# A hybrid attention block on one core: small VectorE instructions rewritten with per-partition scalars, and one DMA issued by another engine

## The chip, the core and the metric

The kernel runs on one core of a Trainium2 chip. That core has TensorE (PE, with PEld for its weight loads), VectorE (DVE), ScalarE (ACT), GpSimd (POOL) and SyncE (SP). Each takes its own stream of instructions in order; they wait for one another through semaphores. DMAs are issued by an engine as one more instruction of its stream: here SP issues most, ACT the rest. The metric is the device time of one execution in microseconds (us), lower is better.

## The reference, cut to what matters

One decoder layer, float32, 2048 tokens, width 1024. After an input projection come 8 forgetting-transformer heads ("fox", 64 wide) and 8 latent-attention heads ("mla", 96 wide for scores, 64 for values), both causal; then an output projection, a squared-ReLU MLP and a final RMSNorm.

```python
def rmsnorm(x, g):
    x32 = x.astype(jnp.float32)
    y = x32 * lax.rsqrt(jnp.mean(x32 * x32, axis=-1, keepdims=True) + EPS)
    return (y * g.astype(jnp.float32)).astype(x.dtype)
...
        logits = jnp.einsum('bhqd,bhkd->bhqk', q_blk, k).astype(jnp.float32) * scale
...
        p = jax.nn.softmax(logits, axis=-1).astype(v.dtype)
        return jnp.einsum('bhqk,bhkd->bhqd', p, v)
```

Two pieces matter here: the softmax of each 128-query row block, whose denominator is a sum of two chunk sums when a row has more than 1024 keys, and the rsqrt of each RMSNorm.

## The kernel before

**Stages.** By the trace: input projection and per-head operand preparation up to about 520 us; attention from about 550 to 1400 us; output projection to about 1650 us; MLP; and final norm to the end.

**Attention.** Units of 512 queries of one head are worked through in the order fox, mla, fox, mla. Three streams of steps are laid over each other by a queue with due times (`SLACK`, `BEHIND`, `STORE`), and a scheduler that simulates the program then sets each engine's order of instructions. For each 128-query tile, PE makes scores (L872), DVE masks them and takes the negative maximum (L877/L880), ACT takes the exponential with its row sum (L881). If a row has two key chunks, `norm` takes their common minimum (L893), two correction factors `fac` on ACT (L894), the sum of `lsum*fac` (L897, L898) and its reciprocal (L899) on DVE; POOL scales the probabilities (L902).

The value product follows: PE transposes four 128x128 blocks of probabilities into one PSUM tile (L922), and `split_ps` divides it into a high part by ACT (L104) and a low part by DVE (L105). PE multiplies the values with the high part (L939) and the low part (L940). So every 512-column product waits for ACT and then for DVE.

**The result of a unit.** The product matrix holds two 64-row parts that are to be added. ACT copies the PSUM result to `o1` (L944); a DMA shifts rows 64 to 127 of it to partitions 0 to 63 of `o2` (L945: "the shift", 128 KB, within SBUF); POOL adds (L950); a DMA stores `o2` to `mixT` (L951). `o2` is one of two buffers, `halves`, taken in turn, so the shift of unit n overwrites the tile that the store of unit n-2 reads, and must wait for that store to land. Shift, store and all loads of the next heads' operands (L197 to L219) are in the stream of SP. A mla head's load is eight DMAs (L206 to L209, twice) into buffers that PE must be done with.

**Norms.** `rstd` computes a reciprocal square root by POOL's power (L80) and one refinement on DVE (L82 to L86), for one column (w=1) or two (w=2).

Of the kernel before, what the change touches and what calls it, by code (L numbers as in the profile page):

```python
# [18 lines left out]
P = 128  # L19
# [26 lines left out]
def block_kernel(ctx, tc, x, positions, attn_norm_g, w_in, b_forget, q_norm_g, w_uq, kv_norm_g, w_ukv,  # L46
# [29 lines left out]
    def rstd(ssq, n, w=1, tag=""):  # L76
        v = sml.tile([P, 4], F32, name=f"rs_v{tag}")[:, 0:w]
        nc.vector.tensor_scalar(v, ssq, 1.0 / n, EPS, ALU.mult, ALU.add)  # L78
        y = sml.tile([P, 4], F32, name=f"rs_y{tag}")[:, 0:w]
        nc.gpsimd.tensor_tensor(y, v, mhalf[:, 0:w], ALU.pow)  # L80
        t = sml.tile([P, 4], F32, name=f"rs_t{tag}")[:, 0:w]
        nc.vector.tensor_tensor(t, y, y, ALU.mult)  # L82
        nc.vector.tensor_tensor(t, t, v, ALU.mult)  # L83
        nc.vector.tensor_scalar(t, t, -0.5, 1.5, ALU.mult, ALU.add)  # L84
        r = sml.tile([P, 4], F32, name=f"rs_r{tag}")[:, 0:w]
        nc.vector.tensor_tensor(r, y, t, ALU.mult)  # L86
        return r

    def rstd_pool(ssq, n, w=1, tag=""):
# [721 lines left out]
    with ExitStack() as es:  # L811
# [36 lines left out]
        def score_steps(head, qb, st):  # L848

            ops, _ = head  # L850
            nch = qb // 2 + 1
            st["p"] = [[] for _ in range(QB)]
            negm = sma.tile([P, QB, nch], F32, name=f"negm{nch}")
            lsum = sma.tile([P, QB, nch], F32, name=f"lsum{nch}")
            fac = sma.tile([P, QB, nch], F32, name=f"fac{nch}")
            steps = []

            def step(j, c):
                t = QB * qb + j
                k0, k1 = cuts(t)[c]  # L860
                w = k1 - k0
                prob = mid([P, 1024])
                st["p"][j].append((k0, prob))
                nb = 1 if w <= 512 else 2
                wb = w // nb
                ps = pss.tile([P, 2, 512], F32, name="ps_s")
                qs = slice(t * P, (t + 1) * P)
                wm = max(wb, 256)
                for i in range(nb):
                    kb = k0 + i * wb  # L870
                    for n, (l, r, rows) in enumerate(ops):
                        nc.tensor.matmul(ps[:, i, 0:wm], l[0:rows, qs], r[0:rows, kb:kb + wm], start=(n == 0),  # L872
                                         stop=(n == len(ops) - 1))
                src = ps[:, 0:nb, 0:wb]
                if c == nch - 1:

                    nc.vector.tensor_tensor_reduce(src, src, maskb[:, 1024 - w:].rearrange("p (b w) -> p b w", b=nb),  # L877
                                                   -1.0, -NEG, ALU.add, ALU.min, negm[:, j, c:c + 1])
                else:
                    nc.vector.tensor_reduce(negm[:, j, c:c + 1], src, AX.XY, ALU.max, negate=True)  # L880
                nc.scalar.activation(prob[:, 0:w].rearrange("p (b w) -> p b w", b=nb), src, AF.Exp,  # L881
                                     scale=-1.0 if c == nch - 1 else 1.0,
                                     bias=negm[:, j, c:c + 1], accum_out=lsum[:, j, c:c + 1])
                if c == nch - 1:
                    norm(j)

            def norm(j):
                rl = sma.tile([P, 1], F32, name="rl")
                if nch == 1:
                    nc.vector.reciprocal(rl, lsum[:, j])  # L890
                else:
                    m = sma.tile([P, 1], F32, name="mmin")
                    nc.vector.tensor_reduce(m, negm[:, j], AX.X, ALU.min)  # L893
                    nc.scalar.activation(fac[:, j], negm[:, j], AF.Exp, scale=-1.0, bias=m)  # L894
                    l2 = sma.tile([P, nch], F32, name=f"l2{nch}")
                    l1 = sma.tile([P, 1], F32, name="l1")
                    nc.vector.tensor_tensor(l2, lsum[:, j], fac[:, j], ALU.mult)  # L897
                    nc.vector.tensor_reduce(l1, l2, AX.X, ALU.add)  # L898
                    nc.vector.reciprocal(rl, l1)  # L899
                for c, (k0, k1) in enumerate(cuts(QB * qb + j)):  # L900
                    pr = st["p"][j][c][1][:, 0:k1 - k0]
                    nc.gpsimd.tensor_scalar(pr, pr, rl, 1.0 if nch == 1 else fac[:, j, c:c + 1], ALU.mult, ALU.mult)  # L902

            for j in range(QB):
                for c in range(nch):
                    steps.append(lambda j=j, c=c: step(j, c))
            return steps

        def value_steps(head, row0, qb, st):
            _, v = head  # L910
            nk = QB * qb + QB
            steps = []

            parts = {}

            def step(kt):
                j0 = max(0, kt - QB * qb)
                o0 = j0 * P
                ps = pspt.tile([P, 512], F32, name="ps_t")
                for j in range(j0, QB):  # L920
                    k0, prob = [p for p in st["p"][j] if p[0] <= kt * P][-1]
                    nc.tensor.transpose(ps[:, j * P:(j + 1) * P], prob[:, kt * P - k0:(kt + 1) * P - k0], ident)  # L922
                if len(due) == 3:
                    due[0]()
                n = turns[0] = (turns[0] + 1) % 3
                hi, lo = place[2 * n], place[2 * n + 1]
                split_ps(hi[:, o0:], lo[:, o0:], ps[:, o0:])
                parts[kt] = hi, lo, o0

                due.append(lambda: product(kt))  # L930

            def product(kt):
                if kt not in parts:
                    return
                due.pop(0)
                if kt == 0:
                    st["o"] = pspt.tile([P, 512], F32, name="ps_t")
                hi, lo, o0 = parts.pop(kt)
                nc.tensor.matmul(st["o"][:, o0:], v[:, kt, :], hi[:, o0:], start=(kt == 0), stop=False)  # L939
                nc.tensor.matmul(st["o"][:, o0:], v[:, kt, :], lo[:, o0:], start=False, stop=(kt == nk - 1))  # L940
                if kt == nk - 1:
                    n = outs[0] = 1 - outs[0]
                    o1, o2 = f32v(place[6 + n]), halves[n]
                    nc.scalar.activation(o1, st["o"], AF.Copy)  # L944
                    nc.sync.dma_start(o2, o1[HD:P])  # L945
                    st["out"] = o1, o2

            def store():
                o1, o2 = st["out"]
                pin(nc.gpsimd.tensor_tensor(o2, o2, o1[0:HD], ALU.add))  # L950
                nc.sync.dma_start(mixT[row0:row0 + HD, qb * 512:(qb + 1) * 512], o2)  # L951

            for kt in range(nk):
                steps.append((lambda kt=kt: step(kt), lambda kt=kt: product(kt)))
            return steps, store
# [529 lines left out]
        return ss  # L1485

    def fin_b(b, half, j, cl, cr, ss):
        nc.vector.tensor_tensor(ss[:, 0:1], ss[:, 0:1], ss[:, 1:2], ALU.add)  # L1488
        r = rstd(ss[:, 0:1], D)
        r0 = 1024 * b + 512 * half + P * j  # L1490
        for side, t in ((0, cl), (1, cr)):
            nc.vector.scalar_tensor_tensor(t[:, j], t[:, j], r, g_f[:, 512 * side:512 * side + 512], ALU.mult, ALU.mult)  # L1492
            nc.scalar.dma_start(out[r0:r0 + P, 512 * side:512 * side + 512], t[:, j])
        if j == 3:
            s8.put(cl, cr)
# [11 lines left out]
    def finish_rows(half, j, at):  # L1507
        rs = slice(512 * half + P * j, 512 * half + P * (j + 1))
        t, r = [], []

        def load():
            t.append(s4.get([P, 1024], F32))
            nc.sync.dma_start(t[0], y0[rs, :])

        def squares():
            ss = sml.tile([P, 2], F32, name="fin_ss")
            for h in range(2):
                nc.scalar.activation(junk, t[0][:, 512 * h:512 * (h + 1)], AF.Square, accum_out=ss[:, h:h + 1])
            r.append(ss)

        def scale():
            ss, = r
            nc.vector.tensor_tensor(ss[:, 0:1], ss[:, 0:1], ss[:, 1:2], ALU.add)
            nc.vector.scalar_tensor_tensor(t[0], t[0], rstd(ss[:, 0:1], D), g_f, ALU.mult, ALU.mult)

        def store():
            nc.sync.dma_start(out[rs, :], t[0])
            s4.put(t[0])

        for n, f in zip((0, 1, 2, 2.5), (load, squares, scale, store)):  # L1530
            when(at + n, f)
# [130 lines left out]
```

## Time and profile before

| | us |
|---|---|
| median of 3 runs | 2899.03 (2896.02 to 2899.87) |
| the profiled execution, its own time | 2889.38 |
| its span, first to last instruction | 2887.5 |
| PE busy | 2782.5 (96%) |
| VectorE busy | 2164.2 (75%) |
| ScalarE busy | 1431.7 (50%) |
| GpSimd busy | 1378.0 (48%) |

The shares are means over stages with different limits; a stage is read from its own stretch. "PEclk" is the granted TensorE clock as a share of full speed, so 0.50 is 1.2 GHz and 1.00 is 2.4 GHz.

### The profile page before, as it was taken

To read this page: it belongs to the slowest core of one execution; us is meant where nothing else is said; L and a number is where in the kernel's file an instruction comes from. 1 tells how busy PE (TensorE), PEld (TensorE's weight loads), DVE (VectorE), ACT (ScalarE), POOL (GpSimd) and SP (SyncE) were. 2 spreads that over 40 slices of the span, in tenths; PEclk is the share of its full clock that TensorE was granted. 3 is DMA by queue.
4 is the path that set the end of the run, shared out by engine and by line. 5 is a ranking of instruction groups with operands and counts; after the bars stand their busy time and mean duration, and the time that the engine had idled before them with its cause. 6 is when DMAs were issued, how large, how long until landed. Compare 5 with 4: busy or idle time off the path is not lost. (4 is left out here: it accounts for less than half of the span.)

```text
span 2887.5 us, 40299 instructions
## 1 busy us (share of the span) xinstructions
PE 2782.5 (96%) x14378; PEld 2366.3 (82%) x14378; DVE 2164.2 (75%) x3313; ACT 1431.7 (50%) x2533; POOL 1378.0 (48%) x1020
## 2 busy tenths in 40 slices
PE   8999999899999999999899999999999999999998
PEld 7878978788888888888778788887887888878886
DVE  6567466588889989989577766676666687997898
ACT  5344352488888888887433332233223433333432
POOL 2726373355555555556532265656556233453421
PEclk9999999899999999999999999999999999999999
DMA  4554544835335344422345644456346744464551
GB/s 140 185 191 164 172 176 155 218 77 123 88 92 116 93 105 112 93 67 61 113 168 194 248 172 160 146 209 227 141 153 225 248 152 152 163 216 172 188 197 59
DMA packets 262968, 442.61 MB, mean 153 GB/s; under 512 B 42416, under 2 KB 150832, under 8 KB 256048
## 3 DMA queue, kind: packets, MB, share of 16 engines
q1 hardware_dynamic: 207296, 300.42, 35.5%
q10 hardware_dynamic: 55472, 139.61, 12.6%
q8 instruction: 114, 1.87, 0.3%
q14 instruction: 86, 0.70, 0.1%
HBM read 275.21 MB, written 156.37 MB: 149 GB/s over the span
## 5 line engine op out<-in xcount | busy, mean ns | idle before, releaser
L1319 PE MATMUL mm<-big,mid 128*128 128x512 f32 x2688 | 614.8, 390 | 3.1 <-ACT big L1394 2.5
L1319 PEld LDWEIGHTS mm<-big,mid 128*128 128x128 f32 x2688 | 504.0, 188 | 112.6 <-ACT big L1394 7.1
L139 PE MATMUL mm<-big,mid 128*128 128x512 f32 x1312 | 513.2, 392 | 8.9 <-DVE mid L248 6.3
L138 PE MATMUL mm<-big,big 128*128 128x512 f32 (+2 forms) x1160 | 436.1, 376 | 2.7 <-DVE big L248 1.7
L872 PE MATMUL ps_s<-big,big 96*128 96x384 f32 (+11 forms) x1720 | 415.8, 366 | 5.8 <-ACT mid L881 5.7
L902 POOL TENSOR_SCALAR mid<-mid,rl,fac 128x768 f32<-128x768 f32 (+4 forms) x256 | 258.4, 1019 | 336.8 <-DVE rl L899 114.7
L137 PE MATMUL mm<-big,big 128*128 128x512 f32 (+2 forms) x1072 | 402.7, 376 | 1.0 <-ACT big L247 1.0
L247 ACT ACTIVATE big<-mid 128x1024 fp32r<-128x1024 f32 x218 | 214.9, 1050 | 316.1 <-PE mm L138 198.0
L881 ACT ACTIVATE mid<-ps_s,negm 128x896 f32<-128x896 f32 (+7 forms) x384 | 332.6, 866 | 59.9 <-DVE negm L877 47.1
L254 POOL TENSOR_TENSOR mid<-mid,mid 128x1024 f32<-128x1024 f32 x88 | 242.8, 2759 | 232.6 <-DVE mid L248 90.5
L922 PE MATMUL ps_t<-ident,mid 128*128 128x128 f32 x2176 | 341.7, 274 | 8.7 <-POOL mid L902 8.3
L922 PEld LDWEIGHTS ps_t<-ident,mid 128*128 128x128 f32 x2176 | 275.2, 142 | 64.0 <-POOL mid L902 10.0
L872 PEld LDWEIGHTS ps_s<-big,big 96*128 96x128 f32 (+2 forms) x1720 | 287.6, 191 | 28.5 <-ACT mid L881 9.2
L1230 POOL TENSOR_TENSOR mid<-mid,mid 128x1024 f32<-128x1024 f32 x60 | 199.0, 3343 | 230.0 <-DVE big L248 206.1
L139 PEld LDWEIGHTS mm<-big,mid 128*128 128x128 f32 x1312 | 247.6, 189 | 63.0 <-DVE mid L248 7.1
L105 DVE TENSOR_TENSOR big<-ps_t,big 128x512 fp32r<-128x512 f32 (+3 forms) x427 | 255.0, 604 | 50.0 <-ACT big L104 46.5
L248 DVE TENSOR_TENSOR mid<-mid,mid 128x1024 fp32r<-128x1024 f32 x112 | 193.2, 1753 | 117.5 <-ACT mid L247 84.3
L104 ACT ACTIVATE big<-ps_t 128x512 fp32r<-128x512 f32 (+3 forms) x427 | 224.6, 536 | 82.2 <-PE ps_t L922 78.2
L138 PEld LDWEIGHTS mm<-big,big 128*128 128x128 f32 x1160 | 219.8, 189 | 39.5 <-DVE big L248 2.6
L877 DVE CUSTOM_DVE_ANT_0 ps_s<-ps_s,maskb 128x768 f32<-128x768 f32 (+7 forms) x256 | 228.2, 892 | 20.1 <-PE ps_s L872 17.8
L137 PEld LDWEIGHTS mm<-big,big 128*128 128x128 f32 x1072 | 203.5, 190 | 33.7 <-ACT big L247 1.9
L247 ACT ACTIVATE mid<-mid 128x1024 fp32r<-128x1024 f32 x112 | 114.2, 1055 | 209.6 <-POOL mid L254 85.1
(227 smaller groups left out, 5309.4 us busy)
## 6 DMA issues: line engine op xcount, KB each, us to landing
gd<-mid ACTq DMA_DIRECT2D x109, 512.0 KB, 2.7
mid<-gd SPq DMA_DIRECT2D x109, 512.0 KB, 4.4
mid<-in_w_up SPq DMA_DIRECT2D x64, 512.0 KB, 5.8
mid<-in_w_down SPq DMA_DIRECT2D x64, 512.0 KB, 4.6
mid<-in_x SPq DMA_DIRECT2D x32, 512.0 KB, 4.0
xd<-mid ACTq DMA_DIRECT2D x28, 512.0 KB, 6.0
big<-xd SPq DMA_DIRECT2D x14, 1024.0 KB, 5.3
mid<-in_w_in SPq DMA_DIRECT2D x24, 512.0 KB, 5.5
```

The costliest lines, as they stand in the source:

```text
L105: nc.vector.tensor_tensor(lo, ps, f32v(hi), ALU.subtract)
L137: nc.tensor.matmul(ps, lh, rh, start=(k == 0), stop=False)
L138: nc.tensor.matmul(ps, lh, rl, start=False, stop=False)
L139: nc.tensor.matmul(ps, ll, rh, start=False, stop=(k == nk - 1))
L247: nc.scalar.activation(hi, raw, AF.Copy)
L254: (eng or nc.gpsimd).tensor_tensor(t, raws[a], raws[b], op)
L872: nc.tensor.matmul(ps[:, i, 0:wm], l[0:rows, qs], r[0:rows, kb:kb + wm], start=(n == 0), stop=(n == len(ops) - 1))
L877: nc.vector.tensor_tensor_reduce(src, src, maskb[:, 1024 - w:].rearrange("p (b w) -> p b w", b=nb), -1.0, -NEG, ALU.add, ALU.min, negm[:, ...
L881: nc.scalar.activation(prob[:, 0:w].rearrange("p (b w) -> p b w", b=nb), src, AF.Exp, scale=-1.0 if c == nch - 1 else 1.0, bias=negm[:, j, ...
L902: nc.gpsimd.tensor_scalar(pr, pr, rl, 1.0 if nch == 1 else fac[:, j, c:c + 1], ALU.mult, ALU.mult)
L922: nc.tensor.transpose(ps[:, j * P:(j + 1) * P], prob[:, kt * P - k0:(kt + 1) * P - k0], ident)
L1319: nc.tensor.matmul(ps[:, m], l[:, k, tk(m)], r[:, :, tk(k)], start=(first and k == n == 0), stop=(k == 3 and n == 2), skip_group_check=True)
```

## The change

Two edits. First, small VectorE instructions that took two tensors (`tensor_tensor`) become `tensor_scalar` instructions, which take one tensor and up to two per-partition scalars (a 128x1 column each). Second, the shift is issued by ScalarE in place of SyncE. Lines of the changed kernel are 3 higher from the end of `rstd` on (L944/L945 become L947/L948, L951 becomes L954, L104 becomes L107, L881 becomes L884).

```diff
@@ rstd
         t = sml.tile([P, 4], F32, name=f"rs_t{tag}")[:, 0:w]
-        nc.vector.tensor_tensor(t, y, y, ALU.mult)
-        nc.vector.tensor_tensor(t, t, v, ALU.mult)
+        r = sml.tile([P, 4], F32, name=f"rs_r{tag}")[:, 0:w]
+        cols = [slice(c, c + 1) for c in range(w)]
+        for c in cols:
+            nc.vector.tensor_scalar(t[:, c], y[:, c], y[:, c], v[:, c], ALU.mult, ALU.mult)
         nc.vector.tensor_scalar(t, t, -0.5, 1.5, ALU.mult, ALU.add)
-        r = sml.tile([P, 4], F32, name=f"rs_r{tag}")[:, 0:w]
-        nc.vector.tensor_tensor(r, y, t, ALU.mult)
+        for c in cols:
+            nc.vector.tensor_scalar(r[:, c], t[:, c], y[:, c], None, ALU.mult)
         return r
@@ norm, in the attention
-                    l2 = sma.tile([P, nch], F32, name=f"l2{nch}")
+                    l0 = sma.tile([P, 1], F32, name="l0")
                     l1 = sma.tile([P, 1], F32, name="l1")
-                    nc.vector.tensor_tensor(l2, lsum[:, j], fac[:, j], ALU.mult)
-                    nc.vector.tensor_reduce(l1, l2, AX.X, ALU.add)
+                    nc.vector.tensor_scalar(l0, lsum[:, j, 0:1], fac[:, j, 0:1], None, ALU.mult)
+                    nc.vector.tensor_scalar(l1, lsum[:, j, 1:2], fac[:, j, 1:2], l0, ALU.mult, ALU.add)
                     nc.vector.reciprocal(rl, l1)
@@ product, the last key tile of a unit
                     nc.scalar.activation(o1, st["o"], AF.Copy)
-                    nc.sync.dma_start(o2, o1[HD:P])
+                    nc.scalar.dma_start(o2, o1[HD:P])
@@ fin_b and finish_rows, alike
-        nc.vector.tensor_tensor(ss[:, 0:1], ss[:, 0:1], ss[:, 1:2], ALU.add)
+        nc.vector.tensor_scalar(ss[:, 0:1], ss[:, 0:1], ss[:, 1:2], None, ALU.add)
```

SP's stream before, at the load of the third mla head (mq, mr, mk and krd are the head's operands in DRAM): eight loads, the store L951 of an earlier unit ahead of the last of them, then two shifts.

```order
L206 DMA big_9438<-mq_79 64x2048
L207 DMA big_9438<-mr_81 32x2048
L208 DMA big_9439<-mk_83 64x2048
L209 DMA big_9439<-krd_77 32x16x128
L206 DMA big_9440<-mq_80 64x2048
L207 DMA big_9440<-mr_82 32x2048
L208 DMA big_9441<-mk_84 64x2048
L951 DMA mixT<-mid_4985 64x512
L209 DMA big_9441<-krd_78 32x16x128
L945 DMA mid_4985<-mid_4984 64x512 x2
```

The same place in the changed kernel: the store stands behind all eight loads, and there is no shift in this stream any more.

```order
L209 DMA big_9430<-mq_79 64x2048
L210 DMA big_9430<-mr_81 32x2048
L211 DMA big_9431<-mk_83 64x2048
L212 DMA big_9431<-krd_77 32x16x128
L209 DMA big_9432<-mq_80 64x2048
L210 DMA big_9432<-mr_82 32x2048
L211 DMA big_9433<-mk_84 64x2048
L212 DMA big_9433<-krd_78 32x16x128
L954 DMA mixT<-mid_4977 64x512 x3
L218 DMA big_9434<-mv 128x16x128
```

ScalarE's stream before, a few instructions after those loads are due: the copy of a unit's result (L944), and behind it splits (L104) and exponentials (L881).

```order
L944 ACTIVATE mid_4984<-ps_t 128x512 [waits DMAHW1_49,PE_49,Pool_49]
L104 ACTIVATE big_4982<-ps_t 128x512 [waits DVE_49,PE_49]
L881 ACTIVATE mid_8480,lsum_8374<-ps_s,negm_8373 128x1024 [waits DVE_49]
L104 ACTIVATE mid_4983<-ps_t 128x512 [waits PE_49,Activation_49]
L881 ACTIVATE mid_8528,lsum_8526<-ps_s,negm_8525 128x128 [waits DVE_49]
```

The same place after: copy, two exponentials, then the shift, which waits on two DMA semaphores (DMAHW3 is raised by the store L954 that follows the eight loads, DMAHW4 by the load of mk ahead of it), and behind it the next splits (L107).

```order
L947 ACTIVATE mid_4976<-ps_t 128x512 [waits DMAHW1_49,PE_49,Pool_49]
L884 ACTIVATE mid_8472,lsum_8366<-ps_s,negm_8365 128x1024 [waits DVE_49]
L884 ACTIVATE mid_8520,lsum_8518<-ps_s,negm_8517 128x128 [waits DVE_49]
L948 DMA mid_4977<-mid_4976 64x512 [waits DMAHW4_49,DMAHW3_49,Activation_49]
L107 ACTIVATE big_4974<-ps_t 128x512 [waits PE_49]
L107 ACTIVATE mid_4975<-ps_t 128x512 [waits PE_49]
L107 ACTIVATE big_4974<-ps_t 128x512 [waits DVE_49,PE_49]
L884 ACTIVATE mid_8529,lsum_8518<-ps_s,negm_8517 128x256 [waits DVE_49]
```

These two pieces stand in the same form at six mla head loads. What moved: the store slid behind one more load, and the shift went from a stream of DMAs into one whose next rows are compute.

## Rows read from the trace of the kernel before

**Rows 1.** Windows by stage: from:to, length, busy of PE/PEld/DVE/ACT/POOL, PEclk, DMA share, GB/s.

```profile
520.00:600.00 80.00, 65.58 (x375) 56.45 (x374) 55.76 (x139) 45.84 (x108) 29.19 (x33) 0.87 0.66 173
...
800.00:1000.00 200.00, 198.93 (x1231) 174.77 (x1231) 178.24 (x458) 165.30 (x382) 107.26 (x110) 1.00 0.43 100
...
1200.00:1405.00 205.00, 194.85 (x1160) 168.31 (x1159) 173.32 (x408) 158.66 (x350) 119.38 (x111) 0.98 0.27 72
1405.00:1650.00 245.00, 230.57 (x1111) 191.29 (x1110) 174.49 (x307) 90.03 (x125) 77.55 (x72) 0.98 0.54 186
```

**Rows 2.** Groups by line on VectorE: count, ns min/median/max, first and last start.

```profile
L897 DVE TENSOR_TENSOR l<-lsum,fac x128: 134/155/3540, 550.4 to 1389.1; 128x2 f32<-128x2 f32 x128
...
L898 DVE TENSOR_REDUCE l<-l x128: 139/146/155, 550.6 to 1392.3; 128x1 f32<-128x2 f32 x128
...
L82 DVE TENSOR_TENSOR rs_t<-rs_y x48: 148/159/2345, 1410.1 to 2882.2; 128x1 f32<-128x1 f32 x32, 128x2 f32<-128x2 f32 x16
...
L84 DVE TENSOR_SCALAR rs_t<-rs_t x48: 141/155/706, 1410.5 to 2882.6; 128x1 f32<-128x1 f32 x32, 128x2 f32<-128x2 f32 x16
...
L78 DVE TENSOR_SCALAR rs_v<-ssq x16: 141/154/156, 1446.1 to 1635.6; 128x1 f32<-128x1 f32 x16
```

**Rows 3.** Timeline of VectorE, 1342:1349: start, length, instruction, [idle before <- releaser].

```profile
1344.21 3.54 DVE L897 TENSOR_TENSOR l<-lsum,fac 128x2 f32<-128x2 f32 x1 [0.75 <-ACT fac L894]
```

**Rows 4.** Timeline of GpSimd, 1340:1350.

```profile
1344.29 1.11 POOL L968 TENSOR_SCALAR mid<-mid,go 128x1024 f32<-128x1024 f32 x1
1345.37 2.35 POOL L970 TENSOR_TENSOR big<-mid,big 128x1024 fp32r<-128x1024 f32 x1
```

**Rows 5.** Waits of 1325:1405: engine and line, who released it, us in total, times, longest.

```profile
PE ps_t L940 <- DVE big L105: 6.7, 5, 3.2
```

**Rows 6.** Windows around two PE stalls (columns as in rows 1).

```profile
1349.00:1354.00 5.00, 5.00 (x24) 4.35 (x24) 4.86 (x9) 2.76 (x6) 5.00 (x5) 0.69 0.13 30
...
1393.00:1398.00 5.00, 4.67 (x17) 3.95 (x18) 2.66 (x5) 1.22 (x2) 5.00 (x4) 0.66 0.14 45
...
1411.00:1417.00 6.00, 3.59 (x22) 2.63 (x21) 5.45 (x6) 2.78 (x5) 3.08 (x2) 1.00 0.67 219
```

**Rows 7.** Timeline of SyncE's DMA queue, 798:822.

```profile
800.48 0.46 SPq L206 DMA_DIRECT2D big<-mq  x1
...
805.16 0.62 SPq L951 DMA_DIRECT2D mixT<-mid  x1
805.83 0.58 SPq L209 DMA_DIRECT2D big<-krd  x1
806.97 9.83 SPq L945 DMA_DIRECT2D mid<-mid  x2
```

**Rows 8.** Waits of SyncE's queue over the span.

```profile
SPq L945 <- DMA mixT<-mid: 71.2, 14, 10.5
```

**Rows 9.** Timeline of ScalarE, 808:819.

```profile
810.13 0.60 ACT L944 ACTIVATE mid<-ps_t 128x512 f32<-128x512 f32 x1 [0.41 <-issue]
811.04 0.60 ACT L104 ACTIVATE big<-ps_t 128x512 fp32r<-128x512 f32 x1 [0.31 <-PE ps_t L922]
```

**Rows 10.** Timeline of PE, 808:819.

```profile
809.88 0.45 PE L872 MATMUL ps_s<-big,big 128*128 128x256 f32 x2
...
812.25 0.47 PE L939 MATMUL ps_t<-big,big 128*128 128x512 f32 x1
```

**Rows 11.** Timeline of ScalarE and its DMA queue, 1751:1766.

```profile
1753.38 8.38 ACTq L1325 DMA_DIRECT2D gd<-mid  x4
1761.81 1.03 ACT L1394 ACTIVATE big<-mm 128x1024 f32<-128x1024 f32 x1 [7.45 <-DVE mid L1338]
```

**Rows 12.** Timeline of GpSimd, 565:575.

```profile
569.50 1.25 POOL L950 TENSOR_TENSOR mid<-mid,mid 64x512 f32<-64x512 f32 x1 [8.13 <-DMA mid<-mid]
```

**Rows 13.** Timeline of PE, 571:573.

```profile
571.77 0.47 PE L922 MATMUL ps_t<-ident,mid 128*128 128x128 f32 x1 [7.05 <-POOL mid L902]
```

**Rows 14.** Window after that wait (columns as in rows 1).

```profile
572.00:577.00 5.00, 5.00 (x19) 4.52 (x19) 2.37 (x4) 3.23 (x7) 2.73 (x5) 0.50 0.11 25
```

More of the change, by code (lines that the diff above doesn't have):

```diff
@@ L1522, in scale @@
             ss, = r
-            nc.vector.tensor_tensor(ss[:, 0:1], ss[:, 0:1], ss[:, 1:2], ALU.add)
+            nc.vector.tensor_scalar(ss[:, 0:1], ss[:, 0:1], ss[:, 1:2], None, ALU.add)
             nc.vector.scalar_tensor_tensor(t[0], t[0], rstd(ss[:, 0:1], D), g_f, ALU.mult, ALU.mult)
```

## The prediction

> **What bounds the kernel now.** I first read the busy times by stage. In attention PE works 198.9 of the 200 us from 800, ScalarE 165, VectorE 178 [rows 1]. PE is the bound there; ScalarE has some 17% of slack and VectorE 11%. Any time for which PE stands still in this stage is lost for good, since PE never has a reserve to catch up with. At the edges it stands still more: 14.4 of 80 us at the start, 10.2 of 205 at the end of attention, 14.4 of 245 in the output projection [rows 1]. So the question is not how busy VectorE or SyncE are, but which of their waits reach PE.
>
> Next, the groups of small VectorE instructions. The two-tensor forms have a normal median but a long tail: 155 ns and up to 3540 for `l` (L897), 159 and up to 2345 in `rstd` (L82) [rows 2]. The reduction of the same `l`, one input, never goes over 155 ns, and a one-column tensor_scalar never over 156 (L78) [rows 2]. The longest stall, 3.54 us at 1344.2, lies exactly over two large GpSimd instructions that end at 1347.7 [rows 3, 4]. So a two-tensor instruction waits for GpSimd to be done, and one input does not.
>
> Last, SyncE's queue. At 800.5 it starts a mla head's eight loads, issues a store behind seven of them at 805.2, then a pair of shifts that keep it until 816.8 [rows 7]. The second shift waits for that store to land, which only happens when the load data ahead of it has gone through; over the span such waits come to 71.2 us in 14 [rows 8]. On SyncE this costs nothing: what stands behind it are more DMAs, not needed yet.
>
> **The change, part by part.** My sum is made against the profiled execution's own time, 2889.4 us, of which 2887.5 is the span. The median shown is 2899.0, 0.3% more; I put the sum of the changes onto the median.
>
> *Small instructions.* Counts and lengths hardly move: `norm` stays at two instructions (128 calls), one-column `rstd` loses one of four, and the 16 two-column calls gain one, 16 x 0.155 = 2.5 us of VectorE in a stage where it is busy 174 of 245 us, so it is hidden. If that cover were gone it would cost the 2.5 us. What matters is whether the tail goes. If it does:
> - At the end of attention the low-part split stands behind the stalled `l`, and PE's product behind the split: 6.7 us in five waits [rows 5]. The next 5 us are run partly at 1.2 GHz, with a granted clock of 0.69 and 0.66 [rows 6], another 5 x 0.31 + 5 x 0.34 = 3.3 us. At 1411 to 1417 PE loses 2.4 us [rows 6], where a two-column `rstd` is stalled. Together 12; bounds 0 (another wait ends there as late) and 14.
> - In steady attention PE loses only about 1 us in 200 to everything [rows 1]. Over some 780 us of it that is 4; I take half as such stalls' share: -2, bounds 0 and -4.
> - In the output projection 14.4 us are lost to many causes [rows 1]; I give the `rstd` stalls -3, bounds 0 and -6. The final norm's stalls have no PE wait that I can price: 0.
>
> The Trainium skill (SBUF — State Buffer, Who interferes with whom) says that a VectorE instruction with two SBUF inputs contends with GpSimd's reads, and one with at most one does not outside the two-port modes; the trace agrees with the 3.54 us. The same section lets tensor_scalar enter such a mode, which speaks against the edit where operands allow it. That is rival D.
>
> *The shift on ScalarE.* SyncE is relieved of 64 issues at no gain to PE. ScalarE gets 64 more instructions with waits, and ScalarE's rows behind them are splits and exponentials that PE needs. That an engine's DMA holds its own compute is in the trace: ScalarE's DMAs L1325 keep their place from 1753.4 to 1761.8, and the copy behind them starts at 1761.8, long after VectorE had made its data [rows 11]. Most of the 64 shifts wait for nothing that is late. Those at six mla loads do. There the store stands in the changed order behind all eight loads, and the shift, two exponentials after its copy, waits for the store.
>
> The price of one, from the load at 800: the copy ends at 810.13 + 0.60 = 810.73 [rows 9], the shift could go at 806.97 + 9.83 - 0.48 (one issue) = 816.3 [rows 7], so 5.6 us later. In the changed kernel the store has one more load ahead of it, and the copy has some ten more PE instructions between it and the loads; I set these two off against each other. Behind the shift come 0.3 us of issue (estimated from the 0.46 to 0.62 us of one issue in rows 7) and a split of 0.60 [rows 9] before PE can go on: 6.5 us after the copy. PE has work in the meantime: the stretch from 809.88 to 812.25 [rows 10], then two score tiles more by the order, about 1 us at 0.45 a pair, so until 2.5 us after the copy. PE idle: 6.5 - 2.5 = 4.0 us. Stalls of this size were followed by about 1.6 us lost to the lower clock [rows 6]. So 5.6 a load, 34 for six. Bounds: 2.0 (no lower clock, PE running 2 us longer on what is ready) gives 12; 7.7 (idle 6, when the extra load is not set off, plus 1.7) gives 46.
>
> *The first unit.* Before, GpSimd's add waited 8.13 us for the first shift [rows 12], PE stood for 7.05 behind it [rows 13] and then ran 5 us at 0.50 [rows 14], 2.5 us lost: 9.5. After, that shift is not queued behind SyncE's loads, but by the order ScalarE meets a semaphore of such a load right behind the first copy and is held about as long as above. 5.6 - 9.5 = -4, bounds -9 and +4.
>
> Sum: 34 - 4 - 12 - 2 - 3 = **+13**. That is 2902 on the execution's own base, and 2899 + 13 = **2912 us** on the median.
>
> **Rivals.**
> - **A, faster: ScalarE's waits don't reach PE.** If PE has 4 us more of ready work at each load, or the store lands before the copy, the blocks cost nothing and the gains stand alone: -12 - 2 - 3 = -17, and up to -9 more at the first unit: 2873 to 2882, with partial blocks up to 2893. For it: ScalarE's slack. Against: PE takes its stream in order, and a split is never more than a few products ahead. It decides below 2.5 us a block: 6 x 2.5 = 15 against gains of 17 + 4 = 21 leaves -6, the least that can be told. The Trainium skill (Trainium Kernel Development and Optimization, Key Constraints) says that DMAs from several engines' queues run on the same 16 DMA engines and only issue time is saved; by that alone the move would be worth nothing on PE, and the sum would be this rival's. Rows 11 show the other side, the wait in the issuer's stream.
> - **B, same:** blocks of 2.5 to 4.5 us, 15 to 27, against gains of 21: 2893 to 2905. That is PE finding a microsecond or two more of ready work than I counted.
> - **C, the forecast:** blocks of 4.5 to 7 us, 27 to 42: 2905 to 2920.
> - **D, slower still: the stalls don't go.** L84 is a tensor_scalar and reaches 706 ns all the same [rows 2]; it has two-column calls, which L78 of `ssq` hasn't, and every new one is one column wide. But none of those has pointer scalars, which may be read like a second tensor. Then 34 - 4 = +30, or the blocks are near their upper bound with the gains kept, 46 - 21 = +25: 2920 to 2936.
>
> **How the numbers follow.** I give C 0.45, A 0.13, B 0.17, D 0.25. The order of the changed kernel shows the wait of six shifts and the compute behind it, and the trace its length; that is why the slower cases have most of the chance. The range from 2893 to 2934 leaves out A and a bit of D. A measurement of this kernel can tell about 0.2%, 5.8 us: faster (below 2893.2) is A, 0.13; same is B, 0.17; slower (above 2904.8) is C and D, 0.70.
>
> **What would show it.** PE idle of about 4 us at each of six places some 105 us apart, from about 708 on, each ended by a split (L107) on ScalarE right behind a shift (L948) whose wait is several us, and a granted clock under 0.8 in the 5 us after. `l` lines (L900, L901) with maxima near 160 ns. No wait of 3 us of PE on L108 between 1325 and 1405. PE busy in 800 to 1000, with two loads, down to about 191 of 200. I would be wrong if the shifts' waits on ScalarE stay under 2 us (A), if PE's idle time there has another releaser, or if the new small instructions keep a tail of microseconds (D).

## The result: 1.0% slower

| | before | changed |
|---|---|---|
| median of 5 runs, us | 2897.86 (2894.64 to 2899.87) | 2925.42 (2920.77 to 2929.96) |
| ratio, 95% interval | | 1.0103 (1.009 to 1.0115) |
| profiled execution, span | 2887.5 | 2926.4 |

The forecast was +13 us, the result is +27.6. The sign and the range held; the size did not. The profiled execution of before lies some 8 us under the median of its timed runs and that of the changed kernel 3 over it. So a difference of two traces is good for where time went, and the medians for how much.

Stages of the changed kernel first (columns as in rows 1).

```profile
520.00:600.00 80.00, 63.51 (x361) 52.42 (x360) 54.84 (x143) 46.45 (x110) 30.36 (x34) 0.89 0.69 178
...
800.00:1000.00 200.00, 189.79 (x1138) 165.51 (x1137) 165.49 (x417) 152.77 (x353) 99.19 (x100) 0.97 0.41 96
```

In steady attention PE, 198.93 of 200 us busy before [rows 1], now stands still for 10 of 200, and part of its busy time is at the lower clock. The waits of PE, longest sum first, name the cause: ScalarE's split.

```profile
PE ps_t L942 <- ACT big L107: 21.6, 5, 5.4
PE ps_t L942 <- ACT mid L107: 17.8, 3, 8.5
```

Eight waits, 39.4 us: six of 4.4 to 5.4 at the mla loads, one of 8.5 at the first unit, one of 2.0 at the end. Now one load. SyncE's queue, as in rows 7:

```profile
806.70 0.47 SPq L209 DMA_DIRECT2D big<-mq  x1
...
810.70 0.59 SPq L212 DMA_DIRECT2D big<-krd  x1
813.87 21.34 SPq L954 DMA_DIRECT2D mixT<-mid  x3
```

ScalarE, as in rows 9:

```profile
817.99 0.59 ACT L947 ACTIVATE mid<-ps_t 128x512 f32<-128x512 f32 x1
...
819.56 0.38 ACT L884 ACTIVATE mid<-ps_s,negm 128x128 f32<-128x128 f32 x1
819.81 0.22 ACT L884 ACTIVATION_READ_ACCUMULATOR mid<-ps_s,negm 128x1 f32 x1
824.30 0.47 ACTq L948 DMA_DIRECT2D mid<-mid  x1
824.82 0.60 ACT L107 ACTIVATE big<-ps_t 128x512 fp32r<-128x512 f32 x1 [4.79 <-issue]
```

PE, as in rows 10:

```profile
819.95 0.83 PE L875 MATMUL ps_s<-big,big 128*128 128x256 f32 x4
825.47 0.80 PE L942 MATMUL ps_t<-big,big 128*128 128x512 f32 x1 [4.68 <-ACT big L107]
```

And the windows behind it:

```profile
825.00:830.00 5.00, 4.53 (x13) 3.31 (x14) 3.34 (x10) 3.05 (x9) 2.02 (x3) 0.50 0.11 26
830.00:835.00 5.00, 5.00 (x29) 4.35 (x28) 3.12 (x6) 3.08 (x7) 2.20 (x3) 0.85 0.11 26
```

Read them as one story. The store is issued behind the eight loads at 813.87. The copy (L947) ends at 818.58, ScalarE does two more exponentials, and then holds still at the shift until 824.30, when the store has landed (its semaphore is complete at 824.24). Note that the profile puts the 4.79 us of idle time before the split down to "issue": the engine stood at a DMA whose wait is its own. PE runs out of ready work at 820.8, goes on at 825.47, and runs at 0.50 (1.2 GHz) for more than 5 us. The load starts again at 919.46, 1032.13, 1144.66 and 1257.78 (the first of the six is at 693.36): a round, from one such load to the next, takes 112.8 us, where it took 105.2 from the load at 800.48 [rows 7] (the other four behind it are at 905.71, 1010.91, 1116.15 and 1221.38). So a load costs 7.5 us, and six cost 45.

The small instructions did what they were to do (columns as in rows 2):

```profile
L900 DVE TENSOR_SCALAR l<-lsum,fac x128: 189/204/215, 556.5 to 1424.4; 128x1 f32<-128x1 f32 x128
...
L901 DVE TENSOR_SCALAR l<-lsum,fac,l x128: 260/269/276, 559.1 to 1429.6; 128x1 f32<-128x1 f32 x128
...
L86 DVE TENSOR_SCALAR rs_t<-rs_y,rs_v x64: 261/271/277, 1443.1 to 2921.1; 128x1 f32<-128x1 f32 x64
...
L87 DVE TENSOR_SCALAR rs_t<-rs_t x48: 138/154/2367, 1443.6 to 2921.5; 128x1 f32<-128x1 f32 x32, 128x2 f32<-128x2 f32 x16
```

No tail above 277 ns is left in the new forms. But each is longer than the 155 ns of before [rows 2]: 204 with one pointer scalar, 270 with two. The one instruction that keeps two columns, L87, keeps its tail of 2.4 us.

### The profile page after: what moved, and what is told of

It reads as the page before. It is cut to its first block, busy times and chain, and to the rows that moved or that the text cites. A ratio compares the mean times of both kernels' runs of the same rounds, so it can differ in the third digit from the quotient of the medians.

```text
span 2926.4 us, 40135 instructions
## 1 busy us (share of the span) xinstructions
PE 2794.7 (95%) x14378; PEld 2375.4 (81%) x14378; DVE 2156.5 (74%) x3289; ACT 1428.4 (49%) x2533; POOL 1375.8 (47%) x1020
## 5 line engine op out<-in xcount | busy, mean ns | idle before, releaser
L905 POOL TENSOR_SCALAR mid<-mid,rl,fac 128x768 f32<-128x768 f32 (+4 forms) x256 | 256.1, 1010 | 342.8 <-DVE rl L902 112.7
L884 ACT ACTIVATE mid<-ps_s,negm 128x896 f32<-128x896 f32 (+7 forms) x384 | 332.7, 868 | 59.0 <-DVE negm L880 39.9
L251 DVE TENSOR_TENSOR mid<-mid,mid 128x1024 fp32r<-128x1024 f32 x112 | 193.9, 1760 | 112.8 <-ACT mid L250 80.5
L107 ACT ACTIVATE big<-ps_t 128x512 fp32r<-128x512 f32 (+3 forms) x427 | 224.6, 535 | 106.3 <-PE ps_t L925 81.8
```

## Experiments

Theory T: ScalarE's wait for the store, at six loads, makes the loss, and the small edits gain a little. Rivals: the small edits cost more than they give; 64 issues on ScalarE cost by themselves; the new order of instructions is just worse. All ratios are to the kernel before, run on the same chip. The edits are to the changed kernel if nothing else is said.

**One part at a time.** First the small edits alone:

```diff
-                    nc.scalar.dma_start(o2, o1[HD:P])
+                    nc.sync.dma_start(o2, o1[HD:P])
```

> The small VectorE edits alone; the shift is on SyncE again. Theory T (six waits of ScalarE for a store make the loss, the small edits gain a little): the six PE stalls with their stretch at half clock go, 7.6 us each or 46 in all, and the gain at the end of attention of about 9 us stays: 2885 to 2892 us where the kernel before has 2898. Rival S (the longer one-column instructions, 204 and 269 ns in place of 155 and 146, cost as much as the tail gave): 2895 to 2902. Rival O (the new order of instructions makes the loss, not the wait): 2910 or more.

Measured: 2879.19 us, ratio 0.9934 (0.9921 to 0.9947), so 17.3 us faster, which is under the forecast of T. PE has no wait above 1.4 us at the loads any more, and a round takes 105.4 us on average (from the load at 691.74 to that at 1218.64, five rounds). So the 7.5 us of a load belong to the shift. Then the shift alone, the kernel before with

```diff
-                    nc.sync.dma_start(o2, o1[HD:P])
+                    nc.scalar.dma_start(o2, o1[HD:P])
```

> The shift on ScalarE alone; the small instructions are those of before. Theory T: six PE stalls of about 4.8 us with some 3 us each from the half clock, and the stalls behind two-tensor instructions stay: 2935 to 2945 us. Rival S: no worse than the changed kernel, 2918 to 2928.

Measured: 2949.24 us, 1.0184 (1.017 to 1.0199), +52.7, some 4 us over the forecast of T. The two parts work against each other, and the move alone is worse than both together. Its own trace has the same waits of PE on the split, and in the second row those behind VectorE that the small edits take away:

```profile
PE ps_t L939 <- ACT big L104: 28.2, 7, 5.8
...
PE ps_t L940 <- DVE big L105: 11.2, 18, 3.2
```

Rival S falls on both runs. On top of the small edits the move costs 27.6 + 17.3 = 45 us, which is the six loads of 7.5. Without them it costs 53; where the other 8 us lie was not taken apart.

**The wait, or the issuing?** Four buffers in place of two, so that a shift waits for a store four units back:

```diff
-                    n = outs[0] = 1 - outs[0]
-                    o1, o2 = f32v(place[6 + n]), halves[n]
+                    c = outs[0] = (outs[0] + 1) % 4
+                    n = c % 2
+                    o1 = f32v(place[6 + n])
+                    o2 = room[3][0:HD, n] if c < 2 else room[3][HD:P, n]
+                    near, far = (o1[0:HD], o1[HD:P]) if c < 2 else (o1[HD:P], o1[0:HD])
                     nc.scalar.activation(o1, st["o"], AF.Copy)
-                    nc.scalar.dma_start(o2, o1[HD:P])
-                    st["out"] = o1, o2
+                    nc.scalar.dma_start(o2, far)
+                    st["out"] = near, o2
...
-                pin(nc.gpsimd.tensor_tensor(o2, o2, o1[0:HD], ALU.add))
+                pin(nc.gpsimd.tensor_tensor(o2, o2, near, ALU.add))
```

> The changed kernel with four buffers for the shifted part in place of two (for two units of four the lower 64 rows are shifted up instead, and added and stored there), so that the shift waits for the store of four units ago. Theory T: all 64 issues stay on ScalarE, none waits long, PE loses none of the six 4.8 us: 2880 to 2892 us. Rival I (64 issues of 0.47 us on ScalarE cost by themselves): 2910 to 2925.

Measured: 2887.08 us, 0.9969 (0.9958 to 0.998). All 64 issues are still on ScalarE; what is gone, but for one at the first unit (below), are the waits ahead of them. The group of the shift's line (min/median/max in ns): its issues, then its semaphore waits.

```profile
L951 ACTq DMA_DIRECT2D mid<-mid x64: 468/468/522, 554.8 to 1427.6; - x64
L951 ACTq EVENT_SEMAPHORE  x63: 17/38/38, 554.8 to 1398.4; - x63
```

In the changed kernel the semaphore waits of the same line reach 6.5 us:

```profile
L948 ACTq EVENT_SEMAPHORE  x64: 17/38/6508, 553.5 to 1468.3; - x64
```

So the wait is the cause, and rival I falls: 64 issues of 0.47 us are 30 us of ScalarE's queue, and PE in 800 to 1000 is busy for 198.09 us again. It is 8 us slower than the small edits alone. In the traces 4.7 us are there by the first mla load (at 696.39, with the small edits alone at 691.74). One difference on the way is the first unit, where PE waits for ScalarE:

```profile
556.03 0.79 PE L942 MATMUL ps_t<-mid,big 128*128 128x512 f32 x1 [7.46 <-ACT mid L107]
```

With the small edits alone PE waits there as well, for GpSimd's scaling (L905), but 6.21 us; so this wait explains little over 1 of the 8 us, and the rest is open. The shift waits there for no store but for a load of a fox head's operand. In the changed kernel it is the same, and the trace names it before the first split behind the first shift:

```profile
553.54 0.51 ACTq L948 DMA_DIRECT2D mid<-mid  x1
554.10 0.60 ACT L107 ACTIVATE mid<-ps_t 128x512 fp32r<-128x512 f32 x1 [8.35 <-DMA big<-fq]
```

**Whose stream?** The shift on GpSimd, two buffers:

```diff
-                    nc.scalar.dma_start(o2, o1[HD:P])
+                    nc.gpsimd.dma_start(o2, o1[HD:P])
```

> The changed kernel with the shift issued by GpSimd, two buffers as before. Theory T says that the wait stands in whichever stream issues the shift, and costs what is queued behind it there: GpSimd is held about 5 us at six loads with the scaling of probabilities behind it, but is busy only half of the time and works ahead of PE, so PE loses 0 to 3 us each: 2888 to 2910 us. Rival E (any compute engine as issuer costs PE the same 7.6 us): 2925 or more.

Measured: 2871.42 us, 0.9912 (0.9899 to 0.9925): 25 us faster than before and 54 faster than with ScalarE as the issuer, under the forecast of T. At the load GpSimd is held as ScalarE was:

```profile
809.03 0.56 POOL L948 DMA_DIRECT2D mid<-mid  x1 [4.97 <-DVE rl L893]
```

The releaser named there is only the one that came last, a reciprocal that ends at 808.69 (808.54 + 0.15). GpSimd's wait for the store's semaphore had lasted until 808.51, 10.0 us after that store was issued at 798.48. But GpSimd works ahead of PE, and PE loses nothing that shows: 196.82 of 200 us busy in 800 to 1000, where the small edits alone have 197.06. The further gain is at the first unit: PE's wait there, 7.05 us before [rows 13] and 6.21 with the small edits alone, is gone. PE is busy for 70.94 of the 80 us from 520, with the small edits alone for 66.21, and the first mla load starts 6.0 us earlier (685.70, 691.74).

**Queue, or full DMA engines?** The shift on ScalarE with two buffers as in the changed kernel, and the store on GpSimd:

```diff
-                nc.sync.dma_start(mixT[row0:row0 + HD, qb * 512:(qb + 1) * 512], o2)
+                nc.gpsimd.dma_start(mixT[row0:row0 + HD, qb * 512:(qb + 1) * 512], o2)
```

> The changed kernel with two buffers and the shift on ScalarE, but the store to mixT issued by GpSimd, right behind its add. Theory Q (the store is late because it stands behind eight loads in SyncE's queue): it lands in a few us, ScalarE's six waits go, 2883 to 2893 us, as with four buffers (2887). Rival B (the store is late because the 16 DMA engines are full of load data, whichever queue it is in): the six stalls stay, 2912 to 2926.

Measured: 2910.47 us, 1.0053 (1.0041 to 1.0066): between the two, but nearly that of B, and the trace of the load at 803.51 speaks for B. The last two rows of its DMA issues, 800 to 826: line, count, size and us from issue to landing.

```profile
mid<-mid ACTq DMA_DIRECT2D x2, 128.0 KB, 9.3
mixT<-mid POOLq DMA_DIRECT2D x1, 128.0 KB, 6.7
```

The store landed 6.7 us after its issue, in place of 10.4, but it was issued 3.3 us later in the load: at 813.95, three scalings of probabilities behind its add, not right behind it. Counted from the load's first issue the shift that waits for it goes at 17.3 us, in the changed kernel at 17.6 (824.30 - 806.70). So the move to another queue gained next to nothing. The first row is the shift of the unit before, issued at 810.38 in ScalarE's queue with no load ahead of it: 9.3 us, where the shortest of its group is 2.2. Both transfers landed as the load's data came to its end; the 16 DMA engines are busy all the time (a share of 1.01 from 812 to 819). A store issued as early as SyncE's was not tried.

That the time is better than B's forecast is the order's doing: two splits (816.70 and 817.18) now stand ahead of the shift on ScalarE, so PE runs out of work 16.0 us after the load's first issue and not 14.1. It goes on no sooner, at 18.9 in place of 18.8. ScalarE is held for 3.5 us instead of 4.8, and PE waits 2.9:

```profile
820.76 0.47 ACTq L948 DMA_DIRECT2D mid<-mid  x1
821.33 0.60 ACT L107 ACTIVATE big<-ps_t 128x512 fp32r<-128x512 f32 x1 [3.53 <-issue]
```

```profile
822.44 0.74 PE L875 MATMUL ps_s<-big,big 128*128 128x512 f32 x2 [2.92 <-ACT mid L884]
```

The windows from there, and those after the fifth load's stall (columns as in rows 1), show the clock's part:

```profile
822.40:827.00 4.60, 4.56 (x17) 3.71 (x18) 2.73 (x9) 2.42 (x6) 2.38 (x4) 0.63 0.01 3
827.00:832.00 5.00, 5.00 (x35) 4.46 (x34) 3.71 (x8) 3.69 (x9) 2.94 (x4) 1.00 0.24 57
...
1151.00:1156.00 5.00, 4.73 (x14) 3.75 (x15) 2.51 (x7) 2.64 (x8) 2.30 (x3) 0.50 0.06 14
```

After 2.9 us of idle PE the low clock is over by 827; in the changed kernel after 4.7 us it still held at 830. The round that begins with this load takes 109.2 us, not 112.8: 1.8 us less of idle PE go with 3.5 us less of time. So a shorter stall is cheaper twice.

**Where the small edits gain.** The kernel before with the norm's two instructions alone, then with `rstd` and the two final sums alone (the sums as in the change):

```diff
...
-                    nc.vector.tensor_tensor(l2, lsum[:, j], fac[:, j], ALU.mult)
-                    nc.vector.tensor_reduce(l1, l2, AX.X, ALU.add)
+                    nc.vector.tensor_scalar(l0, lsum[:, j, 0:1], fac[:, j, 0:1], None, ALU.mult)
+                    nc.vector.tensor_scalar(l1, lsum[:, j, 1:2], fac[:, j, 1:2], l0, ALU.mult, ALU.add)
```

> Only the two instructions in the attention's norm are changed; shift on SyncE, norms and final sums as before. Of the 17 us that all small edits gave, the theory that PE's waits at the end of attention make most of it says 9 to 13: 2884 to 2889 where the kernel before has 2896.5. Rival: the gain is in the projection and the final norm, 2892 to 2898.

Measured: 2891.55 us, 0.9988 (0.9978 to 0.9998), -4.

```diff
-        nc.vector.tensor_tensor(t, y, y, ALU.mult)
-        nc.vector.tensor_tensor(t, t, v, ALU.mult)
...
+        for c in cols:
+            nc.vector.tensor_scalar(t[:, c], y[:, c], y[:, c], v[:, c], ALU.mult, ALU.mult)
...
-        nc.vector.tensor_tensor(r, y, t, ALU.mult)
+        for c in cols:
+            nc.vector.tensor_scalar(r[:, c], t[:, c], y[:, c], None, ALU.mult)
...
```

> Only rstd and the two final sums are changed (norm as before, shift on SyncE). If the small edits add up, this is what norm alone left of the 17 us: 11 to 15 us faster, 2881 to 2886 where the kernel before has 2896. The prediction's split (12 and 2 for norm and what stands behind it in attention, 3 for the projection) says the reverse: 2890 to 2895.

Measured: 2896.32 us, 1.0 (0.9989 to 1.0011), no change. Both forecasts missed: the parts give 4 and 0, together 17. At the end of attention it is the norm that gains, as the prediction had it. PE's waits for the low-part split from 1325 to 1445, 7.3 and 1.8 us before, together 9.1, are 3.1 and 0.7 with the norm edit alone:

```profile
PE ps_t L940 <- DVE mid L105: 3.1, 1, 3.1
...
PE ps_t L940 <- DVE big L105: 0.7, 3, 0.2
```

With `rstd` alone they stay (7.4 and 2.1 from 1325 to 1450). From the sixth mla load to the last `rstd` of the projection (L78 of `ssq`) it is 406.9 us with the norm alone and 415.0 with `rstd` alone, where it was 414.2 before and is 408.1 with all small edits. But the entry into attention came out differently in each: the first mla load starts at 701.43 with the norm alone and at 696.62 with `rstd` alone, at 695.25 before and at 691.74 with all. The window from 500 to 600, norm alone:

```profile
500.00:600.00 100.00, 84.16 (x540) 76.56 (x539) 53.09 (x124) 45.88 (x101) 39.17 (x34) 0.85 0.68 182
```

and with all small edits:

```profile
500.00:600.00 100.00, 86.21 (x570) 77.67 (x569) 61.41 (x148) 52.66 (x119) 42.19 (x40) 0.93 0.75 196
```

The granted clock differs by 0.08 over 100 us, and PE's work by 2 us. What in the edits sets it is open; each edit makes the scheduler sort all engines anew, so a part by itself also gets an order of its own.

**Does GpSimd as issuer need the small edits?** The kernel before with the shift on GpSimd alone:

```diff
-                    nc.sync.dma_start(o2, o1[HD:P])
+                    nc.gpsimd.dma_start(o2, o1[HD:P])
```

> The kernel before with the shift on GpSimd and nothing else. If the move out of SyncE's queue is worth the 8 us by which it beat the small edits alone (the first unit's 6 us PE stall gone), 2886 to 2891; if GpSimd's gain needs the small edits (a two-tensor VectorE instruction that waits for a GpSimd held longer), 2893 to 2900.

Measured: 2904.34 us, 1.0029 (1.0016 to 1.0041): 8 us slower, over both forecasts, although the first unit gains as it does with the small edits and GpSimd (70.50 of 80 us busy). The two-tensor instruction of the norm, in 620 to 1300, now has a tail:

```profile
L897 DVE TENSOR_TENSOR l<-lsum,fac x101: 149/158/3332, 620.1 to 1294.5; 128x2 f32<-128x2 f32 x101
```

Its longest was 769 ns there before, and its busy time grew from 32 to 47 us. PE's waits for VectorE's split grew, in the same stretch from 1.4 and 0.6 us to:

```profile
PE ps_t L940 <- DVE big L105: 9.3, 12, 2.7
PE ps_t L940 <- DVE mid L105: 2.6, 4, 0.9
```

So the gain of a move can hang on the other edit; the sum of the two parts alone does not show that.

**The last two columns, and the best version.** The shift on GpSimd, and L87 per column as well:

```diff
-        nc.vector.tensor_scalar(t, t, -0.5, 1.5, ALU.mult, ALU.add)
+        for c in cols:
+            nc.vector.tensor_scalar(t[:, c], t[:, c], -0.5, 1.5, ALU.mult, ALU.add)
```

> The shift on GpSimd, the small edits, and the one small instruction left with two columns (the refinement's -0.5 and 1.5) made one per column as well. Theory T (only width one keeps clear of GpSimd): its longest falls from 1283 ns to about 160; worth 0 to 4 us: 2867 to 2872, where the same kernel without this edit had 2871.4. Rival (the 16 added instructions cost more than the tail): 2873 to 2876.

Measured: 2866.49 us, 0.9912 (0.9898 to 0.9926). The tail is gone:

```profile
L88 DVE TENSOR_SCALAR rs_t<-rs_t x64: 139/152/156, 1396.0 to 2868.5; 128x1 f32<-128x1 f32 x64
```

In time it can't be told from the kernel without this edit (0.9912 both), so what the tail was worth stays open. With the store on GpSimd too (the edit shown above):

> Shift and store both on GpSimd, small edits with every instruction one column wide. Theory T: nothing that computes waits for a load any more, and GpSimd has room for 64 more issues of some 0.6 us: 2864 to 2872 us. Rival I (the issues delay the scaling of probabilities, and PE): 2875 or more.

Measured: 2872.76 us, 0.9928 (0.9915 to 0.994): between the two forecasts, and no better. With four buffers instead (as above, the shift still on GpSimd):

> Shift on GpSimd, all small instructions one column wide, and four buffers for the shifted part. If GpSimd's wait for a store still costs PE anything, 2860 to 2864; if nothing of it reaches PE, 2865 to 2872, no different from two buffers (2866.5).

Measured: 2867.12 us, 0.9895 (0.9881 to 0.991), the same as with two within some 4 us: no loss from GpSimd's wait for the store shows. These versions are about 1.0% faster than the kernel before, and 2.0% faster than the changed one.

## Why the prediction was right in sign and wrong in size

- **The mechanism** was right: six shifts on ScalarE behind six stores, splits behind them, PE behind the splits. It held in place, releaser and count.
- **The step that failed is the price of one load, 5.6 us.** It measured 7.5. Of this the wait itself was right (5.7 us from the copy's end to the shift, 5.6 forecast). PE's idle time is 4.8 us on average (28.9 over six), 4.0 forecast: PE ran out 2.2 us after the copy, not 2.5, and issue and split took 1.2, not 0.9. The larger miss is the clock, put at 1.6 us after "stalls of this size". The stalls ahead of the two windows [rows 6] were shorter, 2.2 and 3.2 us:

```profile
1348.85 0.79 PE L940 MATMUL ps_t<-big,big 128*128 128x512 f32 x1 [2.22 <-DVE big L105]
...
1393.33 0.79 PE L940 MATMUL ps_t<-big,big 128*128 128x512 f32 x1 [3.17 <-DVE big L105]
```

  After 4.8 us the clock stayed at 0.50 longer. Reckoned as in the prediction, 4.53 x 0.5 = 2.3 us were lost in 825 to 830 and 5 x 0.15 = 0.75 in 830 to 835, 3.0 together; by the rounds it is 7.5 - 4.8 = 2.7. The stalls with the store on GpSimd show the same in reverse. Six times 1.9 is 11 of the 15 us by which the forecast fell short. The bound of 7.7 did hold it.
- **The first unit** was to gain 4. ScalarE was held for 8.4 us there, not "about as long as above", because the load that it waits for lands only then (the split's releaser, above); PE waited 8.45 in place of the 7.05 [rows 13]. There was no gain: against the small edits alone the first mla load starts 1.6 us later (693.36, 691.74). This is the rest of the 15 us and a little more; the parts add up only to within 2 or 3 us.
- **The small edits** were to give 17 (12, 2 and 3) and gave 17.3 together. That is luck: norm alone gave 4 and `rstd` alone nothing, and the traces of before and of the small edits, 7.0 us apart (2887.5 and 2880.5), don't show the split. From the sixth mla load to the end of the projection, where 12 and 3 were to be gained, they show 6.1 us. The 3.5 at the entry into attention was not forecast. In steady attention the -2 did not come: five rounds take 526.9 us in place of 526.1. A new wait of PE's scores for ScalarE's exponentials came in, 8.6 us in six from 620 to 1300, where before no such wait stood:

```profile
PE ps_s L875 <- ACT mid L884: 8.6, 6, 1.4
```

  This row is of the small edits alone; by the rounds the wait cost under 1 us. VectorE's longer instructions are one thing that could make it; it was not tried apart.
- **Rival A** (the waits don't reach PE) is what GpSimd as the issuer does, for a reason that the prediction had for ScalarE: slack ahead of PE. GpSimd has it, ScalarE has not. The Trainium skill (DMA: Bandwidth & Descriptors, Issuing engines are not separate DMA queues) says that DMAs started by different engines run on the same 16 DMA engines, and that starting them from several engines only saves the time it takes to issue them. The landings with the store on GpSimd agree with the first half (17.3 and 17.6 us into the load). The times differ from the second: the same 64 shifts cost 45 us more on ScalarE than on SyncE and 8 less on GpSimd, by what stands behind them.
- **Rival D** (pointer scalars are read like a second tensor) falls: no new form has a tail. The Trainium skill (VectorE: DVE Perf Modes, Mode 2×_2P) asks for an outermost non-unit dimension that is even, or odd and equal in source and destination, before an instruction with one tensor may use both read ports. The traces agree: L87 with two columns reached 2367 ns, and L88 with one, which has no such dimension, never went over 156.
- **One row was misread.** For rows 11 the prediction says that the copy starts long after VectorE had made its data. VectorE's L1338 ends at 1760.93 (1757.51 + 3.42), 0.9 us before the copy, and the last of ScalarE's DMAs wait for it. That the copy stands behind those DMAs is right.

## What to carry to other kernels

A DMA that must wait belongs in a stream where nothing urgent is queued behind it: price its wait by what stands behind it on its issuer, not by the engine's mean busy time. Another queue did not make the late transfer land sooner here. A stall of a PE-bound stage costs more than its length, and the clock's share grows with it, so take its price from a stall of the same length. Test two edits that came together apart and crossed: here the halves of the change gave -17 and +53, and the one on GpSimd was a loss alone and a gain with the other.

## What the runs showed of the hardware that was not expected

- A one-column tensor_scalar on VectorE takes 155 ns with immediates, 204 to 212 with one pointer scalar (L900, L89) and 270 with two (L901, L86), each within 26 ns of spread. So the edit lengthens `norm` from 155 + 146 to 204 + 269 ns, 172 ns each time, and buys the absence of a tail.
- A two-tensor VectorE instruction of 128x2 stalled up to 4.6 us (the shift on ScalarE alone); with the shift on GpSimd and these instructions left as they were, their busy time from 620 to 1300 rose from 32 to 47 us.
- While a mla head's load of 3 MB ran, transfers of 128 KB landed only near the end of its data, whichever queue they were in: a store in SyncE's queue behind the loads after 10.4 us, a store in GpSimd's queue issued 3.3 us later after 6.7, a shift in ScalarE's queue with no load ahead of it after 9.3. The shortest landing of such stores and shifts is 2.2 us.
